# A two-layer hybrid encoder on one core: state-space products after the last gate, output products grouped by shape, parameter loads moved

## The chip, the core and the metric

The kernel runs on one NeuronCore of a Trainium2 chip. Five engines work from queues of their own, each strictly in order: PE (TensorE, matrix products; its weight loads are shown as PEld), DVE (VectorE), ACT (ScalarE), POOL (GpSimd) and SP (SyncE, which here only issues DMAs). The metric is the device time of one execution in microseconds (us). Lower is better.

## The reference

Two layers, 1024 tokens, width 1024, all in float32. In each layer the input is RMS-normalised and goes through one input projection, whose columns feed three token mixers. Their outputs are multiplied by SiLU gates, joined, sent through one output projection and added to the input.

- Branch A: sparse attention, 6 heads of 64. A light indexer scores all keys, a top-k picks 256 of them for each query, and attention runs on those.
- Branch B: a diagonal complex state space (called S5 below), 16 groups of 16 channels, each driving a complex state of 64. With `step = exp(log_step)` the state decays by `exp(a * step)`; `x_t = abar x_(t-1) + bbar u_t`, `y = Re(C x) + D u`, then GELU and a gated linear unit.
- Branch C: multi-head latent attention, 6 heads, with low-rank query and key-value latents.

## The kernel before, in words

Products in full precision are made of three: high by high, high by low and low by high. Every weight is therefore split after its load: ACT copies the high part (`whi`, L153) and POOL or DVE subtracts it to get the low part (`wlo`, L154). `mm3` (L166 to L168) and `proj_step` (L758 to L761) issue the three products; in a gate L166 and L167 use `whi` and L168 uses `wlo`.

A layer runs in this order. First come the projections for keys, indexer, latents and queries. Among them stand the gates, one set of 128 output columns each (`gates`, 48 products of 512 columns), and U, the input of the state space. The order is the string `STEPS = "L5C6Q7U01234"`: the last steps are U and the gates 0 to 4. Beside them DVE and POOL run the indexer and the top-k. Then come 48 attention items (`SEQ`), each two heads of one block of 128 queries: scores, exponentials, transposes, products with the values. Then comes the output projection.

Work that is not on this main line is written as generators and interleaved by a planner. `side(gen)` adds one; `tick(us)` moves a planned clock on, and every generator whose time has come emits its next part and yields the planned time until the next. A projection step ticks by a hundredth of its columns, each eighth of half a gate by 0.64, an attention item by `0.9 * (b + 1)` for block b, 194 in all. The clock only decides in which order instructions are emitted. The order of emission is a priority: a list scheduler then runs a model of the engines and fixes the order in each queue, and places an instruction where its inputs are ready in that model.

The state space is such a generator. `tables_then_s5` is added at the step U (`S5AT`). It loads the tables' inputs (`s5_tables`), then runs `s5`, whose yields are stretched by `S5M = 1.5`. It works on two halves of the groups:

- `static(gh)` builds the tables Ti (on POOL) and Wo (on DVE, L279), waits `ST3`, and then makes the kernel matrix: POOL fills `bd` (L414, L418), 16 pairs of small products make it (L425), 8 DMAs put it into `M`, Ti is transposed on PE (L442), and POOL builds the rotation table R (L264 to L269).
- `chunks(gh)` makes `vr` and `vi` on PE (L471), rotates and scans them on DVE (L479 to L490) and rotates back to X on POOL (L279), then yields `ST2`.
- `outputs(gh)` makes, in two halves q of four groups each, three products for each group: `U M` over 128 rows (L508), and two of X with Wo over the 64 rows of that half (L509, L510). Every one shows in the trace as two passes. GELU follows on ACT and DVE.

After both halves the gated unit follows (L547). The result goes into the chunks 3 and 4 of `mix`, which the output projection reads; `mix_early((3, 4))`, added at item 32, polls until they are there. `residual` loads the input again at item 44 (`WOAT`).

`s5_params` prepares small parameters for both layers: three loads of 8 KB (L292) and some 140 DVE instructions of 16 or 32 columns. Its loads are issued between the first four and the last four tiles of x and their norms are `norm_tile` (L661 to L664). The rest is a side generator from the first projection on; only the first exponential is tied behind the last instruction of the first transposed half (`tc.issue_after(late[0])`).

Of the kernel before, what the change touches and what calls it, by code (L numbers as in the profile page):

```python
# [48 lines left out]
STEPS = "L5C6Q7U01234"  # L49
S5W = (0, 0)  # L50
S5M = 1.5
FT = 0.6
ST2 = 8.0
ST3 = 4.0
GLP = 0
KTP = (0, 0, 0)
# [30 lines left out]
def hybrid_kernel(ctx, tc, A, out, dbg=None, layers=DEPTH):  # L87
    nc = tc.nc
    V, S, G, T = nc.vector, nc.scalar, nc.gpsimd, nc.tensor
# [15 lines left out]
    def ps_s(shape, name="s"):  # L105
        return pp.tile(shape, F32, tag="s", name=name, bufs=BANKS)
# [178 lines left out]
    def s5_params():  # L285

        zp.clear()
        o = page([128, 1024], F32, "s5par")[:, 0:560].rearrange("p (l c) -> p l c", l=2)

        def load(n):  # L290
            t = tiny("s5" + n)
            nc.sync.dma_start(t, A["ssm_" + n].rearrange("l p g -> p l g"))  # L292
            return t
        ar, ai, ls = (load(n) for n in ("a_re", "a_im", "log_step"))
        yield 0.1
        with tc.issue_after(late[0]):
            step = exp_acc(ls, "ze")
        e1, th = tiny("e1"), tiny("th")
        V.tensor_tensor(e1, ar, step, op=ALU.mult)
        V.tensor_tensor(th, ai, step, op=ALU.mult)  # L300
        yield 2.0
        mag = exp_acc(e1, "zm")
        yield 2.0
        sn, cn = sincos(th, "zs")
        yield 2.0
        abr, abi, den, t1, t2, nr = (tiny(n) for n in ("abr", "abi", "den", "t1", "t2", "nr"))
        fr, fi = o[:, :, 264:272], o[:, :, 272:280]
        V.tensor_tensor(abr, mag, cn, op=ALU.mult)
        V.tensor_tensor(abi, mag, sn, op=ALU.mult)
        V.tensor_tensor(den, ar, ar, op=ALU.mult)  # L310
        V.tensor_tensor(t1, ai, ai, op=ALU.mult)
        V.tensor_tensor(den, den, t1, op=ALU.add)
        V.reciprocal(den, den)
        V.tensor_scalar(nr, abr, -1.0, None, op0=ALU.add)
        V.tensor_tensor(t1, nr, ar, op=ALU.mult)
        V.tensor_tensor(t2, abi, ai, op=ALU.mult)
        V.tensor_tensor(t1, t1, t2, op=ALU.add)
        V.tensor_tensor(fr, t1, den, op=ALU.mult)
        V.tensor_tensor(t1, abi, ar, op=ALU.mult)
        V.tensor_tensor(t2, nr, ai, op=ALU.mult)  # L320
        V.tensor_tensor(t1, t1, t2, op=ALU.subtract)
        V.tensor_tensor(fi, t1, den, op=ALU.mult)
        yield 2.0

        er, ei = (o[:, :, 72 * x:72 * x + 72].rearrange("p l (t g) -> p l t g", g=8) for x in range(2))
        w1, w2 = (tiny(n, 64).rearrange("p (l t g) -> p l t g", l=2, g=8) for n in ("w1", "w2"))
        G.memset(er[:, :, 0, :], 1.0)
        G.memset(ei[:, :, 0, :], 0.0)
        V.tensor_copy(er[:, :, 1, :], abr)
        V.tensor_copy(ei[:, :, 1, :], abi)  # L330
        for n in (1, 2, 4):
            bc = lambda z: z[:, :, n:n + 1, :].to_broadcast([128, 2, n, 8])
            cmul(V, er[:, :, n + 1:2 * n + 1, :], ei[:, :, n + 1:2 * n + 1, :], er[:, :, 1:n + 1, :], ei[:, :, 1:n + 1, :],
                 bc(er), bc(ei), w1[:, :, 0:n, :], w2[:, :, 0:n, :])
        yield 2.0

        q = tiny("q0", 32).rearrange("p (l c) -> p l c", l=2)
        sq = tiny("qq", 32).rearrange("p (l c) -> p l c", l=2)
        V.tensor_copy(q[:, :, 0:8], cn)
        V.tensor_copy(q[:, :, 8:16], sn)  # L340
        for i in range(9):
            if i >= 2:
                n = o[:, :, 144 + 16 * (i - 2):160 + 16 * (i - 2)]
            else:
                n = tiny(f"q{i + 1}", 32).rearrange("p (l c) -> p l c", l=2)
            V.tensor_tensor(sq, q, q, op=ALU.mult)
            V.scalar_tensor_tensor(n[:, :, 8:16], q[:, :, 0:8], 2.0, q[:, :, 8:16], op0=ALU.mult, op1=ALU.mult)
            V.tensor_tensor(n[:, :, 0:8], sq[:, :, 0:8], sq[:, :, 8:16], op=ALU.subtract)
            q = n
            if i % 3 == 2:  # L350
                yield 2.0
        rho = o[:, :, 256:264]
        V.tensor_tensor(rho, mag, mag, op=ALU.mult)
        V.tensor_tensor(rho, rho, rho, op=ALU.mult)
        V.tensor_tensor(rho, rho, rho, op=ALU.mult)
        nc.sync.dma_start(s5_d.rearrange("l p c -> p l c"), o)
        yield 1.0
# [23 lines left out]
        Z.update(er=er, ei=ei, Br=Br, Bi=Bi, cr=cr, ci=ci, nci=nci, dd=dd, rot=rot, rho=o[:, 256:264])  # L381
        yield 3.0

    def s5(l, Z, us, yb):

        P2 = lambda name: page([128, 2, 4, 8, 16], F32, name)
        j0, j1 = slice(0, 127), slice(1, 128)
# [13 lines left out]
        def static(gh):  # L401
# [5 lines left out]
            eng.tensor_scalar(Wo[:, 1], Wo[:, 1], -1.0, 0.0, op0=ALU.mult, op1=ALU.add)  # L407
            h["Wf"] = Wf = Wo.rearrange("p x g t c -> p x g (t c)")
            yield ST3


            kt = page([128, 8, 128], F32, "s5k")
# [2 lines left out]
            for x, m in enumerate((Z["Br"], Z["Bi"])):  # L415
                for q in range(2):
                    rs = slice(64 * q, 64 * q + 64)
                    G.tensor_copy(bd[rs, x, :, 32 * q:32 * q + 16], m[rs, ps4])  # L418
            p = ps_tr([128, 4, 128])
# [19 lines left out]
            for x in range(2):  # L439
                p = ps_tr([128, 4, 128])  # L440
# [57 lines left out]
        def outputs(gh):  # L498

            h = H[gh]  # L500
            U, M, X, Wf = h["U"], h["M"], h["X"], h["Wf"]
            g2 = page([128, 8, 128], F32, "s5g")
            for q in range(2):
                p = ps_s([128, 8, 4, 16])
                for i in range(4):
                    g = 4 * q + i
                    rs, pl = slice(64 * q, 64 * q + 64), i
                    T.matmul(p[:, :, i, :], U[:, g, :], M[:, g, :], start=True, stop=False)  # L508
                    T.matmul(p[:, :, i, :], X[rs, 0, pl, :], Wf[rs, 0, pl], start=False, stop=False)  # L509
                    T.matmul(p[:, :, i, :], X[rs, 1, pl, :], Wf[rs, 1, pl], start=False, stop=True)  # L510
                pf = p.rearrange("p t g c -> p t (g c)")
                y2 = scr([128, 8, 64], F32, "gl")
                S.activation(y2, pf, AF.Square)
                V.tensor_scalar(y2, y2, 0.044715, 1.0, op0=ALU.mult, op1=ALU.add)
                V.tensor_tensor(y2, y2, pf, op=ALU.mult)
                S.activation(y2, y2, AF.Tanh, scale=0.7978845608028654)
                V.scalar_tensor_tensor(g2[:, :, 64 * q:64 * q + 64], y2, 1.0, pf, op0=ALU.add, op1=ALU.mult)
                yield 3.0
            yield 1.5
            gt = page([128, 1024], F32, f"s5gT{gh}")  # L520
            for h2 in range(2):
                p = ps_tr([128, 4, 128])
                for i in range(4):
                    T.transpose(p[:, i, :], g2[:, 4 * h2 + i, :], ident)
                S.activation(gt.rearrange("p (j t) -> p t j", t=8)[:, 4 * h2:4 * h2 + 4, :], p, AF.Copy)
                yield 1.0
            yb.append(gt)
# [14 lines left out]
        for o in range(2):  # L542
            for hf in range(2):
                cs = slice(512 * hf, 512 * hf + 512)
                p = ps_s([128, 512], "glu")
# [24 lines left out]
    def side(gen, delay=0.0, behind=0):  # L570

        sides.append([gen, clock[0] + delay, behind])
# [128 lines left out]
    for t in range(8):  # L701
        xp = page([128, 1024], F32, f"x{t}")
        nc.sync.dma_start(xp, A["x"][0][128 * t:128 * t + 128, :])
        xnew.append(xp)
        if t == 3:
            nc.sync.dma_start(cst_, A["c_all"])
            gains = load_gains(0)
            ws.load(2)
            params = s5_params()
            next(params)  # L710
    htok = [norm_tile(x) for x in xnew[0:4]]
    hT = [[], []]
    turnh = turn_h(0, hT, htok, gains[0])
# [6 lines left out]
    for l in range(layers):  # L720
# [13 lines left out]
        Z = {}  # L734
# [427 lines left out]
        us = []  # L1162
# [11 lines left out]


        mixf = {}

        def gates(c):
            g = page([128, 1024], F32, f"gate{c}")
            for hf, cs, ps in channels():  # L1180
                th = scr([128, 512], F32, "th")
                S.activation(th, ps, AF.Tanh, scale=0.5)  # L1182
                V.scalar_tensor_tensor(g[:, cs], th, 1.0, ps, op0=ALU.add, op1=ALU.mult)
            nc.sync.dma_start(gate_d[c], g)
# [3 lines left out]

        def tables_then_s5():
            yield from s5_tables(l, Z)  # L1190
            for d in s5(l, Z, us, yb):
                yield S5M * d
            for o in range(2):
                gate_in(3 + o)
                (G if GLP else V).tensor_tensor(mixf[3 + o], yb[o], mixf[3 + o], op=ALU.mult)
                mixed.add(3 + o)
        if l == 0:
            side(params, 1.0)
        proj_halves(ev_g2)
        proj(ev_iq, tps=range(1, 4), outer="I" not in INNER)  # L1200

# [288 lines left out]
        for i, x in enumerate(STEPS, 8 - len(STEPS)):  # L1490
            at(i)
            if i in QAT:
                next(its)
            if x.isdigit():
                gates(int(x))
            elif x == "U":
                inputs_s5()
            else:
                proj(dict(L=ev_g4, C=ev_g3, Q=ev_g5)[x], outer=x not in INNER)
# [162 lines left out]
```

## Time and profile before

| | us |
|---|---|
| median of 3 runs | 1345.49 |
| lowest and highest run | 1343.35, 1346.81 |
| the profiled execution, its own time | 1338.83 |
| its span, first to last instruction | 1337.1 |

| engine | busy us | share of the span |
|---|---|---|
| PE | 1245.9 | 93% |
| DVE | 877.6 | 66% |
| ACT | 686.1 | 51% |
| POOL | 676.8 | 51% |

The span is the stretch that the rows' times count from. A row of the timeline has start, duration, engine, line, operation, output and inputs, size and count; the brackets give the idle time of the engine before it and what ended that. A row of windows has, for a stretch, the busy time of each engine with its instruction count, then the granted PE clock as a part of 2.4 GHz, then DMA.

### The profile page before, as it was taken

What the parts mean: (1) busy time and instruction counts of PE and PEld (TensorE: products, weight loads), DVE (VectorE), ACT (ScalarE), POOL (GpSimd) and SP (SyncE); (2) the same over time, 40 slices, a digit from 0 to 9 for tenths busy, and PEclk for the clock granted to TensorE, in tenths of its full rate; (3) what the DMA queues carried; (4) which work ended last, traced back from release to release, by engine and by line L of the source; (5) the groups of instructions that cost most, each with busy time, mean ns of one, the idle gap of its engine ahead of it and who ended that gap; (6) DMA issues with size and microseconds to landing.
All of it is one profiled execution on the core that took longest, in us unless ns stands there. A gap on an engine that the chain in (4) does not pass through costs nothing. (4 is left out here: it accounts for less than half of the span.)

```text
span 1337.1 us, 23848 instructions
## 1 busy us (share of the span) xinstructions
PE 1245.9 (93%) x8644; PEld 1055.4 (79%) x8644; DVE 877.6 (66%) x2342; ACT 686.1 (51%) x1565; POOL 676.8 (51%) x1112
## 2 busy tenths in 40 slices
PE   5898999699999999999999989997989999999998
PEld 5896898487788778877899879975767786887787
DVE  4968989934786797741253887996366778776121
ACT  5246753021878778752243666412157786877300
POOL 4789159856431457313347963794760335553210
PEclk9898999897999999999999999998979999999999
DMA  6021232322110100241140013133303010004202
GB/s 220 4 71 28 84 110 80 114 75 91 48 54 18 42 27 13 72 175 41 79 145 14 21 60 111 56 105 91 129 13 95 8 55 20 12 31 156 83 32 95
DMA packets 78491, 92.79 MB, mean 69 GB/s; under 512 B 13536, under 2 KB 61280, under 8 KB 78368
## 3 DMA queue, kind: packets, MB, share of 16 engines
q1 hardware_dynamic: 77216, 87.03, 20.3%
q0 software_dynamic: 1152, 4.19, 1.0%
q8 instruction: 68, 1.11, 0.3%
q14 instruction: 55, 0.45, 0.1%
HBM read 63.53 MB, written 26.50 MB: 67 GB/s over the span
## 5 line engine op out<-in xcount | busy, mean ns | idle before, releaser
L758 PE MATMUL pj<-whi,hh 128*128 128x256 f32 (+1 forms) x608 | 173.8, 286 | 0.0
L761 PE MATMUL pj<-whi,hl 128*128 128x256 f32 (+1 forms) x608 | 172.4, 285 | 0.0
L760 PE MATMUL pj<-wlo,hh 128*128 128x256 f32 (+1 forms) x608 | 172.3, 284 | 0.0
L154 POOL TENSOR_TENSOR wlo<-raw,whi 128x1024 fp32r<-128x1024 f32 (+1 forms) x40 | 96.0, 2412 | 144.2 <-ACT whi L153 123.5
L166 PE MATMUL gt<-hh,whi 128*128 128x512 f32 x320 | 130.8, 409 | 0.0
L168 PE MATMUL gt<-hh,wlo 128*128 128x512 f32 x320 | 128.5, 403 | 0.0
L167 PE MATMUL gt<-hl,whi 128*128 128x512 f32 x320 | 128.4, 401 | 0.0
L758 PEld LDWEIGHTS pj<-whi,hh 128*128 128x128 f32 x608 | 118.0, 194 | 1.1 <-issue 0.2
L760 PEld LDWEIGHTS pj<-wlo,hh 128*128 128x128 f32 x608 | 118.0, 194 | 0.7
L761 PEld LDWEIGHTS pj<-whi,hl 128*128 128x128 f32 x608 | 117.4, 194 | 0.3
L1262 ACT ACTIVATE pt<-s 128x512 f32<-128x512 f32 (+1 forms) x154 | 83.1, 555 | 46.3 <-PE s L1256 34.2
L938 DVE SCALAR_TENSOR_TENSOR acc<-rl,iw,acc 128x384 f32<-128x384 f32 (+5 forms) x84 | 93.9, 1120 | 14.3 <-ACT rl L933 11.5
L166 PE MATMUL po<-whi,mix 128*128 128x512 f32 x256 | 98.5, 392 | 1.6 <-DVE gin L1279 1.6
L168 PE MATMUL po<-whi,mix 128*128 128x512 f32 x256 | 99.6, 390 | 0.0
L167 PE MATMUL po<-wlo,mix 128*128 128x512 f32 x256 | 99.6, 390 | 0.0
L1256 PE MATMUL s<-ident,P 128*128 128x128 f32 x588 | 93.5, 275 | 1.6 <-ACT pt L1262 0.9
L1236 ACT ACTIVATE P<-P,nb,qsc 128x1024 f32<-128x1024 f32 (+7 forms) x96 | 82.4, 863 | 16.6 <-DVE nb L1234 16.5
L1579 DVE TENSOR_TENSOR xn<-xn,po 128x512 f32<-128x512 f32 x32 | 22.0, 687 | 103.3 <-PE po L168 92.0
L1182 ACT ACTIVATE th<-gt 128x512 f32<-128x512 f32 x32 | 19.1, 597 | 134.9 <-PE gt L168 49.4
L1236 ACT ACTIVATE P<-P,nb,asum 128x1024 f32<-128x1024 f32 (+7 forms) x96 | 82.4, 864 | 10.6 <-DVE nb L1234 10.3
L933 ACT ACTIVATE rl<-s 128x512 f32<-128x512 f32 (+3 forms) x160 | 74.1, 541 | 24.0 <-PE s L932 15.9
L1226 DVE TENSOR_SCALAR_CACHE_REDUCE P<-s 128x512 f32<-128x512 f32 (+3 forms) x144 | 74.2, 549 | 15.2 <-PE s L1390 11.4
(453 smaller groups left out, 3633.5 us busy)
## 6 DMA issues: line engine op xcount, KB each, us to landing
raw<-in_w_in SPq DMA_DIRECT2D x32, 512.0 KB, 4.5
gate_d<-gate SPq DMA_DIRECT2D x16, 512.0 KB, 2.9
gin<-gate_d SPq DMA_DIRECT2D x16, 512.0 KB, 4.8
raw<-in_w_out SPq DMA_DIRECT2D x16, 512.0 KB, 6.2
x<-in_x SPq DMA_DIRECT2D x8, 512.0 KB, 4.9
cq_d<-cqs SPq DMA_DIRECT2D x16, 256.0 KB, 2.2
cqT<-cq_d POOLq DMA_DIRECT2D x8, 512.0 KB, 6.9
xn<-in_x SPq DMA_DIRECT2D x8, 512.0 KB, 10.1
```

What stands on the lines that cost most here:

```text
L154: (eng or G).tensor_tensor(lo, raw, f(hi), op=ALU.subtract)
L166: T.matmul(ps, lh, rh, start=start, stop=False)
L167: T.matmul(ps, lh, rl, start=False, stop=False)
L168: T.matmul(ps, ll, rh, start=False, stop=stop)
L758: T.matmul(o, hk, hi[:, k, 0:n], start=kh == 0 and i == 0 and k == 0, stop=False, skip_group_check=True)
L760: T.matmul(o, hk, lo[:, k, 0:n], start=False, stop=False, skip_group_check=True)
L761: T.matmul(o, lk, hi[:, k, 0:n], start=False, stop=kh == 1 and k == 3, skip_group_check=True)
L938: V.scalar_tensor_tensor(a, r[:, 0:nk], w, a, op0=ALU.mult, op1=ALU.add, **({"accum_out": ssum[:, b - 2:b - 1]} if h == 7 else {}))
L1226: V.tensor_scalar(Ps[j][:, c0:c1], p[:, 0:c1 - c0], 1.0, -3.0e38, op0=ALU.mult, op1=ALU.max, accum_out=m)
L1236: S.activation(Ps[j][:, 0:nk], Ps[j][:, 0:nk], AF.Exp, bias=nb[:, j:j + 1], scale=it["scale"][:, j:j + 1], accum_out=sums[:, j:j + 1])
L1256: T.transpose(p[:, i, :], Ps[j][:, 128 * kt:128 * kt + 128], ident)
L1262: S.activation(pt[:, 0:n, :], p[:, 0:n, :], AF.Copy)
```

## The change

The diff does four things. `s5` gets a list `gated`, filled after the last gate is emitted; `static` polls for it after the tables, so that everything after Ti and Wo is emitted behind the last gate. `ST2` goes from 8 to 16. `outputs` issues the four products `U M` of a half first and then the eight with Wo, with one start flag for the bank. `s5_params` is created with the projections, so its loads are emitted at the first tick there, and its first yield goes from 0.1 to 8.

```diff
-ST2 = 8.0
+ST2 = 16.0
...
         ar, ai, ls = (load(n) for n in ("a_re", "a_im", "log_step"))
-        yield 0.1
+        yield 8.0
         with tc.issue_after(late[0]):
             step = exp_acc(ls, "ze")
...
-    def s5(l, Z, us, yb):
+    def s5(l, Z, us, yb, gated):
...
             h["Wf"] = Wf = Wo.rearrange("p x g t c -> p x g (t c)")
             yield ST3
+            while not gated:
+                yield 1.0
...
             for q in range(2):
                 p = ps_s([128, 8, 4, 16])
+                rs = slice(64 * q, 64 * q + 64)
                 for i in range(4):
-                    g = 4 * q + i
-                    rs, pl = slice(64 * q, 64 * q + 64), i
-                    T.matmul(p[:, :, i, :], U[:, g, :], M[:, g, :], start=True, stop=False)
-                    T.matmul(p[:, :, i, :], X[rs, 0, pl, :], Wf[rs, 0, pl], start=False, stop=False)
-                    T.matmul(p[:, :, i, :], X[rs, 1, pl, :], Wf[rs, 1, pl], start=False, stop=True)
+                    T.matmul(p[:, :, i, :], U[:, 4 * q + i, :], M[:, 4 * q + i, :], start=i == 0, stop=False,
+                             skip_group_check=True)
+                for i in range(4):
+                    for x in range(2):
+                        T.matmul(p[:, :, i, :], X[rs, x, i, :], Wf[rs, x, i], start=False, stop=x == 1,
+                                 skip_group_check=True)
...
             ws.load(2)
-            params = s5_params()
-            next(params)
...
         mixf = {}
+        gated = []
...
-            for d in s5(l, Z, us, yb):
+            for d in s5(l, Z, us, yb, gated):
...
         if l == 0:
-            side(params, 1.0)
+            side(s5_params(), 1.0)
...
             if x.isdigit():
                 gates(int(x))
+                if x == STEPS[-1]:
+                    gated.append(True)
```

## Rows read from the trace of the kernel before

**Rows 1.** The profile page, busy time of each engine.
```profile
PE 1245.9 (93%) x8644; PEld 1055.4 (79%) x8644; DVE 877.6 (66%) x2342; ACT 686.1 (51%) x1565; POOL 676.8 (51%) x1112
```

**Rows 2.** Windows: last gates, first state-space outputs, and attention of layer 0.
```profile
240.00:260.00 20.00, 10.75 (x48) 8.00 (x48) 19.52 (x29) 3.12 (x5) 19.80 (x21) 0.94 0.40 131
...
320.00:336.00 16.00, 15.54 (x48) 11.86 (x49) 6.10 (x17) 3.48 (x6) 10.92 (x32) 0.50 0.09 26
...
340.00:580.00 240.00, 232.64 (x2036) 191.23 (x2037) 182.98 (x642) 187.00 (x459) 98.83 (x183) 1.00 0.15 51
```

**Rows 3.** Timeline of PE among the gates of layer 0.
```profile
240.04 0.26 PE L425 MATMUL tr<-zp,s5bd 128*48 128x16 f32 x2 [0.97 <-POOL s5bd L418]
...
247.53 0.26 PE L425 MATMUL tr<-zp,s5bd 128*48 128x16 f32 x2 [1.79 <-POOL s5bd L418]
...
252.18 0.40 PE L167 MATMUL gt<-hl,whi 128*128 128x512 f32 x1
262.47 0.61 PE L425 MATMUL tr<-s5o,s5bd 128*48 128x112 f32 x2 [9.89 <-DVE s5o L279]
```

**Rows 4.** Waits of PE: waiter, releaser, us in total, times, longest.
```profile
PE tr L425 <- DVE s5o L279: 19.8, 2, 9.9
...
PE s L510 <- POOL s5x L279: 6.3, 2, 3.2
```

**Rows 5.** Timeline of POOL in the same stretch.
```profile
234.98 0.41 POOL L414 MEMSET s5bd<- 128x384 f32 x1
...
239.46 0.52 POOL L418 COPY s5bd<-zp 64x64 f32<-64x64 f32 x2
...
246.69 0.79 POOL L418 COPY s5bd<-zp 64x64 f32<-64x64 f32 x2
...
255.33 2.79 POOL L154 TENSOR_TENSOR wlo<-raw,whi 128x1024 fp32r<-128x1024 f32 x1
```

**Rows 6.** Timeline of PE from the end of the gates into attention, layer 0.
```profile
313.60 0.38 PE L508 MATMUL s<-s5m,s5U 128*128 128x128 f32 x2
...
315.54 0.39 PE L1412 MATMUL s<-ka_hi,qA 128*128 128x512 f32 x1
...
316.01 0.39 PE L1412 MATMUL s<-ka_hi,qA 128*128 128x512 f32 x1
...
320.46 0.79 PE L510 MATMUL s<-s5o,s5x 64*128 64x128 f32 x2 [3.19 <-POOL s5x L279]
...
332.42 0.79 PE L1412 MATMUL s<-ka_hi,qA 128*128 128x512 f32 x1
```

**Rows 7.** Timeline of PE's weight loads, second state-space outputs of layer 0.
```profile
409.73 0.29 PEld L509 LDWEIGHTS s<-s5o,s5x 64*128 64x128 f32 x2
409.94 0.30 PEld L510 LDWEIGHTS s<-s5o,s5x 64*128 64x128 f32 x2
...
410.78 0.29 PEld L509 LDWEIGHTS s<-s5o,s5x 64*128 64x128 f32 x2
```

**Rows 8.** Timeline of the start.
```profile
14.19 1.87 POOL L150 TENSOR_TENSOR wlo<-raw,whi 128x800 fp32r<-128x800 f32 x1
...
14.67 1.42 DVE L310 TENSOR_TENSOR zp<-zp 128x16 f32<-128x16 f32 x1 [5.35 <-DMA zp<-in_ssm_a_re]
...
17.64 0.47 PE L683 MATMUL tr<-ident,jk 128*128 128x128 f32 x1 [6.72 <-DVE jk L664]
...
21.27 0.50 PE L758 MATMUL pj<-whi,hh 128*128 128x200 f32 x1
```

**Rows 9.** Timeline of DVE among the gates: two table products.
```profile
254.45 4.22 DVE L279 TENSOR_TENSOR s5tab<-zp 128x512 f32<-128x512 f32 x2
```

**Rows 10.** Timeline of layer 0: last gated unit, residual loads, first output product.
```profile
464.27 1.88 PE L547 MATMUL glu<-s5gT,wglu 128*128 128x512 f32 x4
...
561.46 6.79 SPq L1523 DMA_DIRECT2D xn<-in_x  x8
...
586.66 0.48 PE L166 MATMUL po<-whi,mix 128*128 128x512 f32 x1
```

## The prediction

> **What bounds the kernel.** I read the page first. PE is busy 93% of the span [rows 1], so what counts is where PE stands still, and where it runs at the lower clock. The windows show both, at the places that the change touches [rows 2]. From 240 to 260 us PE works 10.75 of 20 us, while DVE and POOL are full (19.52 and 19.80). From 320 to 336 us PE looks busy, but it has the lower of its two clocks (0.50, 1.2 GHz), and 48 product records fill 16 us. In attention, 340 to 580 us, PE is busy 232.64 of 240 us at full clock: there nothing can be gained but by taking work away.
>
> The timeline names what stops PE among the gates [rows 3]. Three times the state space's small products (L425) stand in PE's queue ahead of gate products and wait: 0.97 and 1.79 us for POOL's `bd`, 9.89 us for DVE's table Wo. That is 12.65 us in layer 0. The view of waits counts the long one twice, 9.9 us at most and 19.8 in all [rows 4], so layer 1 repeats it; so it does with the wait of L510 on POOL further on (3.2 us at most, 6.3 in two).
>
> **Part 1: the gates.** The change takes these products out of the gates' stretch. I do not book 12.65 us. The last product before the long stop is a gate's L167 [rows 3], and next in that gate comes L168, which needs `wlo`. POOL makes a `wlo` from 255.33 to 258.12 [rows 5], inside the stop, and I take it to be this gate's. So PE would have stopped there anyway, until 258.12.
>
> After the change PE comes to that point sooner: at 252.58 (252.18 + 0.40), less 2.76 us of waits, less about 0.8 us for state-space products that leave, so near 249.0. POOL loses the three `bd` rows, 0.41 + 0.52 + 0.79 = 1.72 us [rows 5], so `wlo` ends near 256.4. The new stop is 7.4 us; of 12.65 us idle 5.2 goes. I take 5. Bounds: 12.65 if the scheduler puts `wlo` early enough; 3 if POOL gains nothing (249.0 to 258.12 is 9.1 us idle, 3.5 saved, rounded down).
>
> The other products that move (L425, L442, L471) cost PE in attention what they cost here, so they are zero in the sum. Their cover on other engines is treated in part 3.
>
> **Part 2: the outputs.** From 313.60 to 332.42 PE does the first half's outputs with four pairs of attention scores between them [rows 6]. A pair at full clock takes 0.47 us (315.54 to 316.01), four 1.9. So the outputs cost 18.8 - 1.9 = 16.9 us, with a 3.19 us wait for POOL's X in it. After that four score pairs run until 336.0 at the lower clock still [rows 2, 6]: 3.6 us in place of 1.9, 1.7 lost.
>
> The second half's outputs stand in the middle of attention and run at full clock. One cycle of three products takes 1.05 us there (409.73 to 410.78), eight cycles 8.4 us [rows 7]. Within the cycle L510 follows L509, same shape, after 0.21 us (409.73 to 409.94); the other two steps change the shape and share 0.84, so 0.42 each. Grouped, a half q has 12 products: 10 steps of 0.21 and 2 of 0.42, 2.9 us. Four such halves in a layer are 11.8 us.
>
> After the change both halves' outputs are emitted inside attention, and `ST2` gives POOL 12 more planned us to finish X. So the nearest row is the second half's, and I take full clock for both: 16.9 + 1.7 + 8.4 - 11.8 = 15.2 us saved in a layer. If grouping brings nothing, four halves cost 16.8 us, and 10.2 is saved. That is the lower bound; 15.2 serves as the upper one too.
>
> **Part 3: what attention has to take.** About 50 planned us of state-space work join it: two scans and six products on DVE, R and X on POOL, 8 DMA issues for `M` on SP, ahead of the `gin` loads. POOL has room (98.83 of 240 busy) and DVE some (182.98) [rows 2]. The `M` issues stand before the first attention items in SP's queue instead of among the gates; who waits for SP there are the `qa` loads, which are issued some items ahead. I book nothing for them; if that cover is gone, one start slips by some 6.8 us, what eight residual loads take to issue [rows 10].
>
> DVE's moved instructions with two inputs in SBUF (L482, L486 and the scans, four in a layer) may be held. The only such rows that were clearly held took 4.22 us for two, 2.1 each [rows 9]. So 0 to 8.4 us a layer; PE idles only 7.4 of 240 us while it already carries one such set, so I take 2, near the lower end.
>
> **Part 4: the start.** DVE's queue has the parameters' first product (L310) ahead of the norms of tiles 2 and 3. It waits 5.35 us for its load; behind it wait the norms, and for them PE waits 6.72 us, until 17.64 [rows 8]. The first projection product starts at 21.27, so 3.6 us after. After the change these loads are emitted behind the norms. Then `wlo` is the last input: 14.19 + 1.87 = 16.06. The gain is at most 21.27 - 16.06 = 5.2 us. At least it is 0, should the parameters' 140 or so small instructions take it back from DVE later in the same projection. I take 4. I exclude a loss, as DVE's instructions stay the same in number and only come later. The first yield of 8 costs nothing that I can see: the parameters' store is read only at the step U, more than 150 us later.
>
> **Sum.** 4 + 2 x (5 + 15.2 - 2) = 40.4 us. The profiled execution's own time is 1338.8, its span 1337.1; 1338.8 - 40.4 = 1298.4. The median of the runs lies 6.7 us above the profiled one, so for the median: 1345.5 - 40.4 = **1305**.
>
> With the bounds: at best 5.2 + 2 x (12.65 + 15.2) = 60.9, so 1284.6; at worst 0 + 2 x (3 + 10.2 - 8.4) = 9.6, so 1336.
>
> **Rivals.**
>
> *DVE and POOL hold each other up in attention.* The mechanism is the held pair of rows 9: with POOL full, two products took 4.22 us. If all four moved instructions cost 2.1 us and PE waits each time, 2 x (8.4 - 2) = 13 us come back: 1318. For it: those two rows. Against it: POOL was busy 19.80 of 20 us there [rows 2] and is under half busy in attention. I give it 0.12. The Trainium skill, page "SBUF — State Buffer", section "Who interferes with whom", states such a rule: a DVE instruction with two SBUF inputs and a POOL instruction that reads SBUF share a port pair under an exclusive lock, and whichever starts second waits for the whole of the other. By that rule every moved instruction that meets a POOL one pays, which speaks for this rival; the pair of rows 9 agrees with it.
>
> *The products stay where they were.* The scheduler places by readiness in its model. Where its PE waits for `wlo`, it may fill the hole with small products of lower priority, and these wait again in the real queue. Then the gates give nothing and only the grouping and the start are left: 2 x 2 x (8.4 - 5.9) = 10 and 4, so 1331. For it: the stop of rows 3 lies just at such a hole. Against it: `bd` is now emitted late, so POOL fills it late in the model too. I give it 0.08.
>
> *Slower: the output projection waits for chunks 3 and 4.* The state space resumes 50 planned us later, and the two longer yields add 2 x 12: 74. Attention's 194 planned us took 586.66 - 313.60 = 273 us, 1.4 for one, so the gated unit, whose last rows end at 466 us, comes 104 us later: 570 in old time, 16 us before the first output product [rows 10]. Still to come then are the `gin` loads, which stand in SP's queue behind the residual loads (6.79 us to issue), two multiplications and two splits. If buffers for the residual come free only at the end of attention, all of this slips behind it. It decides once the tail is late by more than 20 us in a layer; at 25 us the time is 1305 + 50 = 1355. For it: the margin is 16 us. Against it: the main line is 18 us per layer shorter only at its front, and the residual found its buffers 25 us before the end. I give it 0.07.
>
> **How the numbers follow.** The forecast, with its bounds 1284.6 to 1336, has 0.68; 0.05 is left for what I don't see. 1284 to 1334 holds the forecast, the first two rivals and little else, some 8.5 in 10 after allowance for the edges; it is also the likeliest case's own range. About 0.3% (4 us) is what a measurement can tell from no change. Faster: nearly all of the forecast and of the first two rivals, 0.87. Slower: the third and a part of the unseen, 0.08. Same: 0.05.
>
> **What would show it.** In the changed profile no L425 stands between gate products; PE's idle time before the last gates is about 7 us, ended by POOL's `wlo`; the clock stays 1.00 through the first 20 us of attention; L508 to L510 take about 3 us for each half; the first L758 starts near 17. I am wrong if PE waits at the output projection for `mix`, if DVE is full in attention, or if the long stop stays.

## The result: 1.7% slower, and the profile after

The changed kernel takes 1367.24 us (median of 4 runs, 1364.42 to 1368.07); the kernel before, run beside it, 1344.42 (4 runs, 1341.53 to 1346.81). The ratio is 1.0167, with an interval of 1.0141 to 1.0193. The prediction of 1305 us and its range are missed, on the other side. The profiled execution took 1366.77 us, its span is 27.9 us longer than before.

Two lines of the page after:

```profile
span 1365.0 us, 23837 instructions
...
PE 1257.6 (92%) x8644; PEld 1061.4 (78%) x8644; DVE 885.9 (65%) x2342; ACT 688.2 (50%) x1565; POOL 676.3 (50%) x1112
```

Against [rows 1] PE is busy 11.7 us more, although the grouped outputs take less time, and it idles some 16 us more. Both are net: attention has more of either, the stretch before it less. The windows after; the first two answer to [rows 2], the last two are attention of layer 0 split at the first product with the values of branch C. The items before that are mostly those of branch A ("A items" below), the ones behind it those of branch C ("C items"), whose keys and queries are made while they run.

```profile
240.00:260.00 20.00, 11.64 (x44) 9.20 (x43) 19.83 (x25) 2.60 (x5) 14.97 (x10) 0.83 0.47 140
340.00:580.00 240.00, 221.27 (x1817) 179.98 (x1813) 164.80 (x565) 163.71 (x414) 103.71 (x218) 0.96 0.13 41
294.00:443.00 149.00, 137.86 (x1192) 110.05 (x1192) 105.63 (x372) 109.69 (x263) 59.73 (x131) 0.98 0.13 37
443.00:598.00 155.00, 137.33 (x1060) 110.61 (x1058) 106.12 (x326) 95.35 (x233) 69.81 (x126) 0.92 0.18 61
```

The same two stretches of attention before:

```profile
314.00:474.00 160.00, 151.60 (x1199) 119.31 (x1198) 113.62 (x375) 111.05 (x264) 66.47 (x130) 0.95 0.13 42
474.00:587.00 113.00, 110.20 (x982) 94.20 (x982) 84.23 (x314) 90.12 (x224) 52.65 (x101) 1.00 0.21 74
```

The gates end 20 us earlier (294 in place of 314) and the A items are 11 us shorter. Then the C items take 155 us in place of 113. In these 155 us the clock is 0.92 and PE stands still for 17.7 us (155 - 137.33); before, it was 1.00 and 2.8 us. No engine is full there: DVE is busy 68%, POOL 45%, ACT 62%.

The timeline of PE, and one row of POOL, at the places that the prediction priced (the rows answer to [rows 8], [rows 3], [rows 5], [rows 7] and [rows 10]):

```profile
14.28 0.54 PE L760 MATMUL pj<-whi,hh 128*128 128x200 f32 x1
16.24 0.53 PE L762 MATMUL pj<-wlo,hh 128*128 128x200 f32 x1 [1.43 <-POOL wlo L150]
...
239.96 0.39 PE L167 MATMUL gt<-hl,whi 128*128 128x512 f32 x1
248.70 0.79 PE L168 MATMUL gt<-hh,wlo 128*128 128x512 f32 x1 [8.36 <-POOL wlo L154]
...
245.78 2.87 POOL L154 TENSOR_TENSOR wlo<-raw,whi 128x1024 fp32r<-128x1024 f32 x1
...
363.98 1.06 PE L509 MATMUL s<-s5m,s5U 128*128 128x128 f32 x8
364.97 2.05 PE L513 MATMUL s<-s5o,s5x 64*128 64x128 f32 x16
...
598.53 0.48 PE L166 MATMUL po<-whi,mix 128*128 128x512 f32 x1
```

And the view of waits for PE, over the whole run (it answers to [rows 4]):

```profile
PE s L1391 <- DVE P L1229: 18.6, 8, 4.2
PE gt L168 <- POOL wlo L154: 16.7, 2, 8.4
PE acc_o L1252 <- ACT pt L1265: 9.4, 8, 2.7
...
PE s L509 <- DVE s5g L521: 4.8, 2, 2.6
...
PE tr L1348 <- DVE kt L1341: 4.3, 3, 2.1
```

The state space's small products no longer stop the gates; `wlo` does, as forecast. New at the top is a score product of the C items (L1391) that waits for DVE's row maxima (L1229). Two such stops, in the timelines of DVE, POOL and PE:

```profile
457.38 0.72 POOL L266 TENSOR_TENSOR s5R<-s5tab 128x256 f32<-128x256 f32 x1
458.13 0.69 DVE L481 TENSOR_TENSOR s5tab<-vr,s5R 128x512 f32<-128x512 f32 x1 [2.90 <-POOL s5R L266]
458.74 0.68 DVE L1229 TENSOR_SCALAR_CACHE_REDUCE P<-s 128x512 f32<-128x512 f32 x1
459.49 0.38 PE L1391 MATMUL s<-kc1h,qT 104*128 104x256 f32 x1 [3.96 <-DVE P L1229]
...
584.80 2.35 DVE L1198 TENSOR_TENSOR gin<-s5gT,gin 128x1024 f32<-128x1024 f32 x2
587.07 0.55 DVE L1229 TENSOR_SCALAR_CACHE_REDUCE P<-s 128x384 f32<-128x384 f32 x1
587.68 0.47 PE L1391 MATMUL s<-kc1h,qT 104*128 104x128 f32 x1 [3.45 <-DVE P L1229]
```

In the first, DVE's queue has a state space step (L481) ahead of the row maxima. It waits 2.90 us for POOL's R, and PE, whose next score needs the bank that the row maxima free, stands 3.96. In the second the step ahead is not waiting, it is long. The windows around the two show what follows:

```profile
456.00:460.00 4.00, 0.52 (x4) 0.52 (x5) 1.87 (x6) 0.00 (x0) 3.77 (x7) 1.00 0.00 0
460.00:464.00 4.00, 4.00 (x21) 4.00 (x21) 4.00 (x11) 2.22 (x7) 1.00 (x4) 0.59 0.00 0
584.00:588.00 4.00, 0.55 (x3) 0.36 (x3) 3.70 (x7) 1.87 (x2) 0.75 (x1) 0.87 0.00 0
588.00:592.00 4.00, 3.17 (x12) 2.37 (x12) 3.93 (x14) 2.42 (x7) 3.94 (x2) 0.50 0.00 0
```

PE is nearly idle in one window and at or near the lower clock (1.2 GHz) in the next. So these two stops are paid twice.

**One table for all that follows.** From PE's timeline, layer 0: the front is from 0 to the end of the last gate product, attention from there to the first output product. Attention is split into the state space's products, all other products (the same work in every kernel, 1980 records) and idle time; each is the sum of the rows, overlaps counted once. The last column is the C items' part of it. Attention of layer 1 agrees within 4 us unless said.

| kernel | ratio to before | front | attention | state space | other | idle | C items |
|---|---|---|---|---|---|---|---|
| before | 1 | 313.8 | 272.9 | 35.7 | 226.0 | 11.2 | 112.5 |
| after | 1.0167 | 293.7 | 304.8 | 33.1 | 242.9 | 28.8 | 155.8 |
| e1 | 0.9805 | 307.6 | 266.4 | 27.5 | 226.6 | 12.3 | 112.8 |
| e2 | 0.9880 | 295.2 | 283.2 | 32.3 | 236.2 | 14.6 | 133.6 |
| e5 | 1.0107 | 305.4 | 286.1 | 27.6 | 236.4 | 22.2 | 136.2 |
| e7 | 1.0059 | 296.3 | 290.8 | 32.0 | 237.5 | 21.3 | 122.1 |
| e18 | 1.0115 | 295.0 | 299.7 | 34.6 | 239.6 | 25.5 | 143.0 |

Layer 0 is 11.8 us longer: 20.1 less in the front, 31.9 more in attention. In layer 1 it is 11.7 less and 27.7 more. Of layer 0's loss in attention 17.6 us are idle time, and 16.9 are other products that take longer for the same work. By the granted clock, 25.8 us of these products ran at the lower of the two clocks, against 3.5 before; at half the speed, 22.3 us more there cost some 11 us. So the clock is about two thirds of the 16.9. The remaining 6 are spread over all kinds of products, and no run explains them.

### The profile page after: what moved, and what is told of

Read it like the earlier page. It is cut to its first block, busy times and chain, and to the rows that moved or that the text cites. A ratio compares the mean times of both kernels' runs of the same rounds, so it can differ in the third digit from the quotient of the medians.

```text
span 1365.0 us, 23837 instructions
## 1 busy us (share of the span) xinstructions
PE 1257.6 (92%) x8644; PEld 1061.4 (78%) x8644; DVE 885.9 (65%) x2342; ACT 688.2 (50%) x1565; POOL 676.3 (50%) x1112
## 5 line engine op out<-in xcount | busy, mean ns | idle before, releaser
L168 PE MATMUL gt<-hh,wlo 128*128 128x512 f32 x320 | 128.1, 402 | 16.7 <-POOL wlo L154 16.7
L940 DVE SCALAR_TENSOR_TENSOR acc<-rl,iw,acc 128x384 f32<-128x384 f32 (+5 forms) x84 | 93.4, 1114 | 14.9 <-ACT rl L935 11.8
L1259 PE MATMUL s<-ident,P 128*128 128x128 f32 x588 | 98.7, 286 | 4.4 <-DVE mx L1231 1.3
L168 PE MATMUL po<-whi,mix 128*128 128x512 f32 x256 | 99.5, 389 | 0.0
L1231 DVE CUSTOM_DVE_ANT_0 P<-s,bias 128x512 f32<-128x512 f32 (+3 forms) x144 | 77.0, 553 | 16.1 <-PE s L1416 15.3
L168 PEld LDWEIGHTS gt<-hh,wlo 128*128 128x128 f32 x320 | 62.5, 195 | 31.1 <-POOL wlo L154 17.6
```

The source lines that it names most:

```text
L168: T.matmul(ps, ll, rh, start=False, stop=stop)
L940: V.scalar_tensor_tensor(a, r[:, 0:nk], w, a, op0=ALU.mult, op1=ALU.add, **({"accum_out": ssum[:, b - 2:b - 1]} if h == 7 else {}))
L1231: V.tensor_tensor_reduce(Ps[j][:, c0:c1], p[:, 0:c1 - c0], bi[:, c0:c1], 1.0, -3.0e38, ALU.add, ALU.max, m)
L1259: T.transpose(p[:, i, :], Ps[j][:, 128 * kt:128 * kt + 128], ident)
```

## Experiments

The median of the kernel before lay between 1337.4 and 1344.4 us on different occasions, so kernels are compared by their ratios to the kernel before as it ran beside them; 0.01 is 13.4 us.

**The parts alone.** e1 is the changed kernel without the wait and with the old `ST2`; e2 keeps the wait. e3 and e4 are the kernel before with only the diff in `outputs`, and only the moved parameters.

```diff
-ST2 = 16.0              # e1, e2
+ST2 = 8.0
-        gated = []      # e1
+        gated = [True]
```

> The changed kernel without its wait for the last gate and with ST2 back at 8: only the grouping and the moved parameters remain. Place theory (the loss is the second half of the state space, which the wait and ST2 push into the last third of attention, the C items, where it makes PE stand still 15 us a layer and leaves it 10 us a layer at the lower clock): the C items take about 113 us a layer again instead of 155, PE idles under 4 us in them, and with the start (7 to 8 us, kept) and the grouping (about 9 us of PE a layer) the time is about 1320 us. Grouping theory (issuing the U M products first makes PE wait for a bank or for X): the C items may be short, but the outputs now hold PE for longer than before, and the time is 1345 or above.

> The changed kernel with ST2 back at 8, the wait for the last gate kept: 24 planned us less delay for the second half. Place theory: the second half still begins behind the last gate, but its scans and outputs come earlier, about a third of the planned delay is gone, so a part of the 43 us that the C items take longer comes back: 5 to 15 us a layer, time 1337 to 1357. Rival (ST2 alone makes the loss, the wait is harmless): C items near 113 us, time about 1300. Second rival (the wait alone makes it): time stays within 4 us of 1367.

> The kernel before with the grouped outputs as its only edit. Place theory: state space products on PE fall from 42 us a layer to about 33, half of this lies on the path of PE or all of it, so 9 to 18 us faster: 1327 to 1336. Grouping theory: PE waits in the grouped outputs for X or a bank, time 1345 or more.

> The kernel before with the moved parameter loads as its only edit. The first projection product starts near 14 us instead of 21; if nothing takes it back the time falls by 7 to 8 us, to about 1338. Rival: the 140 small DVE instructions come back later in the same projection and the time is within 3 us of before.

Measured beside a median of 1337.79: e1 1314.79 (ratio 0.9774 to 0.9837), e2 1323.90 (0.9847 to 0.9912), e3 1324.55 (0.9850 to 0.9916), e4 1330.83 (0.9899 to 0.9955). The grouping is worth 13 us and the parameters 7; together they give 23, so these two parts are what is good in the change, and **e1 beats both kernels**. The wait costs 9 us net (e2 against e1), and `ST2` 0.9880 to 1.0167, some 38 us. The grouping theory falls on the time, though e3 has a wait of its kind (3.11 us, shown further on), and my forecast for e2 falls too: a doubled yield does more harm than the wait for the gates. Attention of e1:

```profile
308.00:461.00 153.00, 143.55 (x1198) 115.31 (x1196) 114.69 (x375) 110.72 (x264) 67.36 (x130) 0.97 0.14 42
461.00:574.00 113.00, 110.14 (x980) 93.91 (x979) 84.30 (x313) 90.46 (x226) 52.70 (x101) 1.00 0.21 74
```

The C items are as before the change, to the microsecond.

**Where the second half lies.** e5 has the longer yield without the wait; e6 and e7 keep the wait and shrink all yields of the state space.

```diff
-ST2 = 16.0              # e5, beside gated = [True]
+ST2 = 15.0
-S5M = 1.5               # e6 (1.1), e7 (1.0 and ST2 = 8.0)
+S5M = 1.1
```

> The changed kernel without its wait for the last gate, and with ST2 at 15 (in place of 16): the longer yields alone. Place theory (what costs is how much of the state space's second half falls into the C items): without the wait the second half ended at 467 us in e1, some 6 us into the C items; 2 x 7 x 1.5 = 21 planned us later it ends near 490 to 500, so the gated unit and a part of the outputs lie in C, as in e2: C items 118 to 130 us, time 1320 to 1340. Rival (the longer yield is bad by itself, wherever it puts the work, since e2 against the changed kernel gives 43 us to it): about 1315 + 40 = 1355.

> The changed kernel with wait and ST2 = 16 both kept, but all yields of the state space stretched by 1.1 in place of 1.5, so that its second half comes earlier by about a quarter of the stretch between the last gate and its end. Place theory: the rows of R of the second half lie at 385 to 410 us instead of 428 to 459, the outputs near 460 to 475, so the C items take 115 to 135 us and the time is 1310 to 1335. Rival (the wait for the gates or the length of ST2 is what costs): 1350 to 1367.

> The changed kernel with ST2 = 8 and the state space's yields stretched by 1.0: behind the last gate, but packed closer. Place theory: the second half is done about when the C items begin, C 113 to 120 us, and the shorter front of the changed kernel is kept: 1300 to 1315, at or below e1. Rival (packed closer it holds up the A items, which run at the same time): A items 5 to 10 us longer than in e2, time 1320 or more.

Measured beside 1337.43: e5 1350.82 (1.0090 to 1.0123), e6 1343.83 (1.0013 to 1.0056), e7 1345.24 (1.0042 to 1.0075). All three are slower than the place theory allows. e5 lies near its rival: the longer `ST2` costs 0.030 without the wait (e5 against e1) and 0.029 with it (the changed kernel against e2), so it does its harm by itself. In e5 only the last transposes and the gated unit (together 8.7 us on PE) and the multiplications lie beside the C items, yet these take 136 us. e6 lies between its two forecasts. In e7 the state space's last step ends at 468.9 us, when the C items have just begun (465), and they take 122; there the A items pay, 168.7 us against 149.6 in e2, which differs from e7 only in the stretching, and 153.6 in e1. That is e7's rival. So it is not the C items alone: **in none of the places tried did attention take these steps for nothing**. Wherever more of the state space was moved in, PE's idle time and its time for the other products rose against e1 (the table).

**One stop taken away.** e8 moves the two multiplications of the second stop shown above to POOL.

```diff
-                (G if GLP else V).tensor_tensor(mixf[3 + o], yb[o], mixf[3 + o], op=ALU.mult)
+                G.tensor_tensor(mixf[3 + o], yb[o], mixf[3 + o], op=ALU.mult)
```

> The changed kernel with one step moved: the two multiplications of the gates' chunks 3 and 4 with the state space's result (2 x 1.2 us) go from DVE to POOL. In the changed kernel they stand on DVE ahead of the row maxima of a C item, and PE stands still 3.45 us for these (587.68 and 1256.50 us), and runs at the lower clock for some 7 us after. In-order theory (each step of the state space on DVE delays the C item queued behind it): this stop goes with its low clock, 4 to 7 us a layer, so 1353 to 1359. Rival (PE would stand there anyway, for the next late input): within 4 us of 1367.

Measured: ratio 1.0191 (1.0174 to 1.0208), so no gain on 1.0167. In place of the stop of 3.45 us stand two of 1.17 and 1.18 us, for the next late inputs: the rival's case.

**Buffers.** The state space's data live in a pool of 40 pages of 4 KB and in two rings of scratch buffers (K1, K2) that attention uses too, so a later end also holds these longer. e9 has fewer scratch buffers, e10 with them one page more, e11 and e12 two pages fewer.

```diff
-K1 = 6                  # e9, e10
+K1 = 4
-K2 = 5
+K2 = 4
-PAGES = 40              # e10: 41; e11 (of after) and e12 (of e1): 38
+PAGES = 41
```

> The changed kernel with two small scratch buffers of each of two sizes fewer (K1 6 to 4, K2 5 to 4) and 40 pages as before: the base for the run with 41 pages. Every theory: 1360 to 1385, as the scratch is used by the gated unit and the query preparation.

> As the run before, with the room freed given to one page more (41 in place of 40). Page theory (the state space holds its pages of 4 KB longer, and attention's loads and key tiles wait for a free one): clearly faster than the base, 8 us or more, and the waits in the C items get shorter. Place theory (it is the order of the queues): within 4 us of the base.

> The changed kernel with 38 pages in place of 40. Page theory: 16 us slower or more, 1383 and above, with SP's loads of queries and weights issued later still. Place theory: within 6 us of 1367.

> The fast version without wait and with ST2 = 8 (e1), with 38 pages in place of 40. Page theory: even without the delay there is hardly a page to spare, so it gets slower by 8 us or more and shows stops in the C items like those of the changed kernel. Place theory: within 4 us of 1315.

Measured: e9 1.0457 (1.0425 to 1.0488), e10 1.0411 (1.0380 to 1.0443), e11 1.0292 (1.0254 to 1.0330), e12 0.9967 (0.9953 to 0.9982). e9 itself missed its range (1401.0 us). Pages are short everywhere: two fewer cost 17 to 22 us, and one more gives 6 (e10 against e9), less than the page theory's 8. But not where the change lost its time: the C items of e10 take 167.3 and 168.4 us, those of e9 171.5 and 165.4, so a page more does not shorten them clearly. With two pages fewer they stay short in e12:

```profile
469.00:583.00 114.00, 110.19 (x976) 93.80 (x976) 83.36 (x312) 89.75 (x224) 52.66 (x101) 1.00 0.20 70
```

They take 114 us, as in e1, and in e11 148.8 and 158.5 (two layers), near the 155 with 40 pages. Pages are not what lengthens the C items. Scratch looked better, as e9's C items are longer than the 155 of the changed kernel, and the trace of the changed kernel has a wait of a scratch writer for PE's reads of an older scratch buffer (view of waits, ACT; then PE's wait for the row maxima in e13):

```profile
ACT qj L1364 <- PE tr L1348: 10.9, 4, 3.8
```

```profile
PE s L1391 <- DVE P L1229: 16.8, 5, 5.1
```

e13 has nine scratch buffers of 2 KB in place of five (and 38 pages, so e11 is its base). e14 to e16 load `wglu`, which sits in one of the five throughout, only behind `outputs(1)`.

```diff
-PAGES = 40              # e13
+PAGES = 38
-K2 = 5
+K2 = 9
...
-        wg = scr([128, 2, 256], F32, "wglu")      # e14 (after), e15 (e2), e16 (e1)
-        nc.sync.dma_start(wg, A["ssm_w_glu"][l].rearrange("(k p) c -> p k c", p=128))
...
         yield from outputs(1)
+        wg = scr([128, 2, 256], F32, "wglu")
+        nc.sync.dma_start(wg, A["ssm_w_glu"][l].rearrange("(k p) c -> p k c", p=128))
```

> The changed kernel with 38 pages and nine scratch buffers of 2 KB (K2) in place of five; e11, with 38 pages and five, is its base (1379 us). Scratch theory (the key and query preparation of the C items and the state space take turns in five scratch buffers, and what writes one waits until PE has read the other's): the waits of ACT's qj and kt for PE's transposes go, the C items fall from about 153 us a layer to 120 to 138, of which 17 are the state space's own products, and the time to 1320 to 1350. Place theory (strict order of the queues alone): within 8 us of 1379.

> The changed kernel with the load of wglu, which holds one of the five scratch buffers from the start of the state space on, moved behind the second half's outputs. Scratch theory: attention has five buffers instead of four to share through the C items up to the gated unit: 10 to 30 us faster, 1337 to 1357. Place theory: within 4 us of 1367, or slower, as the gated unit may wait for its load.

> The same late load of wglu in e2 (wait for the last gate kept, ST2 = 8, 1324 us). Scratch theory: e2 has 20 us a layer more in its C items than e1, 14 of them the state space's products; some of the rest goes: 1308 to 1320. Place theory: within 4 us of 1324.

> The same late load of wglu in e1 (no wait, ST2 = 8, 1315 us), where the state space has left the scratch buffers when the C items begin. Both theories: within 5 us of 1315, with C items near 113 us; if scratch bound the A items too, it would be faster by more.

Measured: e13 1.0217 (1.0172 to 1.0262), e14 1.0199 (1.0157 to 1.0241), e15 0.9899 (0.9858 to 0.9940), e16 0.9927 (0.9900 to 0.9953). In e13 the waits of `qj` and `kt` for the transposes are gone, and the C items take 147.7 and 148.5 us, against 148.8 and 158.5 in e11. Scratch is worth some 5 us a layer, 1 in one and 10 in the other; the wait for the row maxima stays, 16.8 us. With 0.0075 gained on e11, e13 fits neither of its forecasts. e14 and e15 gained nothing on their bases (1.0167 and 0.9880). The scratch theory falls as the main cause. e16 missed in its own way: one load moved made e1 slower by 0.0122, 16 us. In the profiled executions, 8.6 us apart, the A items take 159 us against 153. One new stop there is 1.84 us of PE at 454.26 us: it waits for row maxima, which stand on DVE behind a product of the gated unit (L564) that took 2.84 us beside two splits on POOL (5.11 us) and 0.69 in e1. The rest has no cause that I found. It also says how far a verdict on a single small edit goes here: one load moved can change the time by 1%.

**The queues.** e17 builds the second half's R with the tables Ti and Wo, so that DVE need not wait for it among the C items. e18 leaves the second half's R, its DVE steps on `vr` and `vi`, the scans and X out; two ACT copies stand in their place.

```diff
             h["Wf"] = Wf = Wo.rearrange("p x g t c -> p x g (t c)")     # e17
+            if gh == 1:
+                yield from rtable(h, ps4)
...
+            if gh == 1:                                                # e18, behind vr and vi
+                h["X"] = X = page([128, 2, 4, 128], F32, "s5x")
+                for x, d in ((0, vr), (1, vi)):
+                    S.activation(X[:, x], d, AF.Copy)
+                yield 8 * FT + 5.0
+                yield ST2
+                return
```

> The changed kernel with one step of the second half earlier: its rotation table R (POOL) is emitted with the tables Ti and Wo, some 40 us before the C items, in place of behind the kernel matrix. In the changed kernel POOL makes R from 428 to 459 us among the ropes of the C items, and DVE's first product with R waits 2.9 us for it with the row maxima of a C item behind it (PE stands 3.96 us and runs at the lower clock after). In-order theory (state space steps on POOL and DVE stand ahead of C items' steps): this stop goes with its clock, C falls by 6 to 12 us a layer, the time to 1343 to 1357. Scratch theory: C stays, within 4 us of 1367. If A grows by what C loses, within 4 us too, and the next late input has taken over.

> The changed kernel without the second half's rotation: R, the eight DVE steps on vr and vi, the two scans and X on POOL are left out (vr and vi go to the outputs unrotated, through two ACT copies); all products of PE, the GELU, the gated unit and the yields stay. In-order theory: with these some 40 steps gone from POOL's and DVE's queues the stops at 449 to 490 us go, C falls by 12 to 25 us a layer, the time to 1320 to 1345. Rival (what costs is PE's own part, 17 us of state space products beside the C items, and their banks): C falls by under 6 us a layer, the time stays above 1355.

Measured: e17 1.0181 (1.0152 to 1.0211), e18 1.0115 (1.0085 to 1.0146). In e17 the stop of 3.96 us is gone and the C items fall by 7.9 and 6.8 us, as forecast; but the A items, which now have R beside them, grow by 4.3 and 4.9, and no gain is left that can be measured. The C items of e18:

```profile
452.00:595.00 143.00, 134.36 (x1071) 110.53 (x1068) 95.33 (x315) 94.80 (x233) 49.56 (x99) 0.93 0.21 70
```

They fall by 12.8 and 14.7 us, inside the forecast, and idle time in them halves (17.7 to 8.6 us); the A items grow by 7.6 and 9.5. The time falls by 0.0052, 7 us, in place of 22 or more. Most of the A items' growth is one stop, just ahead of the line that divides A from C:

```profile
439.58 4.88 POOL L154 TENSOR_TENSOR mix<-gin,mix 128x1024 fp32r<-128x1024 f32 x2
439.83 2.44 DVE L1356 TENSOR_TENSOR kt<-kr,kr__5888 128x128 f32<-128x128 f32 x1
442.19 2.29 DVE L1252 SCALAR_TENSOR_TENSOR nb<-mx,qsc 128x2 f32<-128x2 f32 x1
445.88 0.58 PE L1406 MATMUL s<-kc0h,qT 104*128 104x256 f32 x1 [5.12 <-DVE P L1244]
```

Two short DVE steps (the first took 0.28 us at 444.94) took 2.44 and 2.29 us while POOL split two chunks of `mix`, and the row maxima stood behind them. All of these are attention's own. So the steps on POOL and DVE in the queues ahead of the C items do make stops there, about a third of the C items' loss, but attention as a whole gains only 5.1 us a layer of its 31.9 and 27.7 without them, as another late input takes their place. How the rest divides between PE's own part (17.3 us in the C items, the gated unit among it) and the stops of the GELU and the multiplications stays open.

## Why the prediction was wrong, point by point

**The start** was booked at 4 us, at most 5.2. e4 shows 7. The norms did come sooner, and `wlo` comes at 16.24, near the 16.06 forecast. But the bound was wrong: I let the first product wait for `wlo`, and it reads `whi`. So it starts at 14.28, 7.0 us earlier, and only the next product waits for `wlo`, 1.43 us. What follows keeps the gain: the first gate product starts 7.9 us earlier (104.8 in place of 112.7).

**The gates** were right. Forecast was a stop of 7.4 us before L168, ended by `wlo`; it is 8.36. PE came there at 240.35 and `wlo` ended at 248.65; with the 8 us of the start taken off, the forecast (249.0 and 256.4) reads 241.0 and 248.4. The idle time of the front fell by 4.2 us in layer 0 and 6.0 in layer 1 (e2 against e1), 5 was booked.

**The outputs.** A grouped half was to take 2.9 us; from 363.98 to 367.02 it is 3.04. The sum was too high: 15.2 us a layer were booked, e3 gives 13.2 for both layers. PE's own time for the state space fell by 8.3 us a layer in e3 (41.9 to 33.6). But the wait for X stays, 1.79 us, and behind the first outputs PE stands for a score product until DVE ends the GELU; the clock is 0.50 from 322 to 330 us there. I had priced no such wait:

```profile
325.96 0.77 PE L1414 MATMUL s<-ka_hi,qA 128*128 128x512 f32 x1 [3.11 <-DVE s5g L519]
```

I had also counted on full clock once the outputs came later. In the changed kernel the second half's outputs wait 2.25 us for the GELU before them and run at the lower clock (0.53 from 532 to 539), and some 20 us into attention the clock falls without any outputs: PE waits 2.72 us for ACT's `pt` at 314.71, and the clock is 0.50 from 316 to 320.

**Attention: the step that failed.** Part 3 let attention take all the moved work for 2 us a layer, 0 to 8.4 at most, and Part 2 took `ST2` as a gift ("gives POOL 12 more planned us to finish X") and priced nothing behind it. Measured: attention grew by 31.9 and 27.7 us in the two layers although the outputs in it became cheaper. The error has three parts. First, I priced a moved DVE instruction only by its being held by POOL, 0 to 2.1 us; the additions that I named took 0.66 to 0.69 us and the scans 1.20 to 1.90 (before: 1.21 to 1.82), so none of these was held for long. What moved steps cost is that they wait in the queue (2.90 us for R) or just stand there, ahead of the row maxima that free PE's banks. Second, I read 232.64 busy of 240 [rows 2] as "there nothing can be gained but by taking work away"; it also means that there is little slack to hide a new wait in. Third, I left the clock out of this part: some 11 of the 31.9 us are the same products at the lower clock. What the runs show is that the wait and `ST2` together make the whole loss (e1, without both, is the fastest), and that a third of what the C items lost goes when the second half's steps on POOL and DVE are left out (e18); how the remainder divides is open.

**The rivals.** DVE and POOL did hold each other up in attention, as the first rival had it, in these rows:

```profile
446.38 2.35 POOL L154 TENSOR_TENSOR mix<-gin,mix 128x1024 fp32r<-128x1024 f32 x1
446.45 2.56 DVE L1340 TENSOR_TENSOR kt<-kt,kr__5916 128x256 f32<-128x256 f32 x1 [0.85 <-POOL kr__5916 L163]
449.19 0.47 DVE L1340 TENSOR_TENSOR kt<-kt,kr__5916 128x256 f32<-128x256 f32 x1
```

The same step took 2.56 us beside POOL's and 0.47 without. The Trainium skill, page "SBUF — State Buffer", section "Who interferes with whom", gave this rival its rule: a DVE instruction with two SBUF inputs waits for the whole of a POOL instruction that reads SBUF. The trace agrees with it. PE's stop of 2.06 us at 449.32 was for these keys. POOL also held moved steps, but not those that the prediction counted: of the gated unit's four products (L564), which now lie beside the C items, two took 2.63 and 2.74 us and two 0.69 and 0.67. One of them, with POOL's split:

```profile
566.08 2.36 POOL L154 TENSOR_TENSOR mix<-gin,mix 128x1024 fp32r<-128x1024 f32 x1 [7.03 <-ACT mix L153]
566.35 2.63 DVE L564 TENSOR_TENSOR s5gT<-th,s5gT 128x512 f32<-128x512 f32 x1 [0.43 <-PE glu L551]
```

So this holding acts on attention's own steps and on moved ones, also with POOL busy 45% of the time. No run here prices it apart. The second rival fell: no L425 (now L427) stands between gate products. The third rival, the slower one, had the time line nearly right: it put the end of the gated unit 16 us ahead of the first output product, and the multiplications behind it end at 587.15 (row 584.80), 11 us ahead of that product at 598.53. Its mechanism did not happen: PE waits 0.8 us for the last input there, as in the kernel before. I had worked out how late in attention the state space would end, and asked only whether it ends in time, not what it stands in front of. That the change came out slower, as this rival said, is no merit of it.

## What to carry to other kernels

Work moved from a stretch with idle engines into one where the bounding engine is 97% busy is not free because the other engines have room: price each moved step by what is queued behind it on its engine, and count in the lower clock where it follows the stop. Before a planner's delays are lengthened, follow the whole tail of the delayed unit and write down beside which work it comes to lie. Run the parts of a change alone: here two of four were worth 23 us and the other two hid that.

## What was not expected of the hardware

The lower clock can follow short stops. Behind a stop of 1.47 us (489.55 us in the changed kernel) the clock was 0.50 from 492 to 494, and behind the stops of 2.06 to 3.96 us in its C items it was at the lower level for some 3 to 7 us each time. But not every stop brings it: PE stands 1.77 us before 572.39 in the kernel before, where the C items have 1.00 throughout, and in e6 it stands 2.36 us before 503.94, with 1.00 from 504 to 512. So the length of a stop alone does not tell here whether it is paid twice.
